# Two-layer streaming trunk: order of the second gate's products and stores, priority of the last block's evictions, place of the last transposes, start of the weight ring

## The chip, the cores and the metric

The kernel runs on one core of a Trainium2 chip as one program. The metric is the device time of one execution in microseconds (us), given as the median of several runs. Engines are named as in the profile: PE is the matrix engine, PEld its weight loads, DVE the vector engine, ACT the scalar engine, POOL the GpSimd engine, and SP the queue that issues most DMAs.

## The reference, cut to what matters

The trunk has two layers on 1024 positions of 1024 channels, in float32. Layer 0 mixes tokens with an S5 state-space mixer and a GLU, layer 1 with a short gated convolution. After each mixer come a SwiGLU feed-forward network with 2816 hidden units and a gated embedding:

```python
def swiglu_ffn(u, w_in, w_out):
    gate, up = jnp.split(u @ w_in, 2, axis=-1)
    return (jax.nn.silu(gate) * up) @ w_out

h = x
for i in range(DEPTH):
    hn = rmsnorm(h, norm_mix_g[i])
    mix = s5_mixer(hn, ...) if i % N_MIXERS == 0 else shortconv_mixer(hn, ...)
    h = h + mix
    h = h + swiglu_ffn(rmsnorm(h, norm_ffn_g[i]), ffn_w_in[i], ffn_w_out[i])
    gate = jax.nn.sigmoid(rmsnorm(h, norm_ple_g[i]) @ ple_w_gate[i])
    h = h + gate * (p[i] @ ple_w_up[i])
return rmsnorm(h, final_norm_g)
```

## The kernel before

**Products.** Every float32 operand is kept as two reduced-precision halves, high and low. `split` makes them: ACT casts the high half (L90), DVE subtracts it from the source (L91). One product of two operands is three matmuls (`mm3`, L124 to L126). On top of that the feed-forward input product works on 2x2 blocks with seven block products instead of eight (`block_product`). Product i of a block uses operand i of seven weight operands, and twelve matmuls. The seven results are added up in three PSUM tiles and in SBUF: L362 copies product 0 out on ACT, and DVE evicts products 1, 2, 4, 5 and 6 in L366, L370, L374, L376 and L378. Products 4, 5 and 6 start over in a PSUM tile that L366, L370 and L374 have emptied; they wait for those.

**Stages.** After the S5 mixer and the GLU (to about 400 us) comes the feed-forward input of layer 0, called f0: 22 blocks, in eleven pairs (one gate of a pair is `product(j)`, the other `product(j + NK)`). Then comes its output product `ffn_out`, then the gated embedding, the convolution, and the same feed-forward for layer 1, f1.

**A pair's hidden values.** Each pair yields seven operands for the output product. `store` splits one into a tile `hs` of a ring of four (tag by tag in turn) and sends it to DRAM (`hw`) with a DMA of POOL's queue (L473). Stores 0 and 1 belong to the first block of the pair. Stores 2, 6, 3, 4 and 5 belong to the second. Store 2 needs `u0`, which the seventh product completes (L378); store 6 needs `u1`, which the sixth completes (L376). With four tiles, store 5 takes the tile of the store that stands four places ahead of it in the text.

**The hand-over to the output product.** The last of the 22 blocks runs with `beside`: between its products, two generators (`make`) turn raw rows of the output weights into the operands of the first group of `ffn_out`, on ACT and DVE. Each makes four subtractions (L537, L541, L546, L549); the first generator does them on DVE, the second on POOL. The operands lie in `ulow` and `uhigh`, over the activations that the block has finished with. `ffn_out` takes its hidden values back from DRAM in chunks, four tiles `s8t` in turn, and the rows of `h` likewise; the list `queued` keeps these loads in one order on SP. The tiles of `s8t` and `h` lie where the ring of nine weight operands `ws` and the `hs`, `ev` and `kept` tiles lie, so a load waits until the last user of that place is done.

**`ffn_out`.** Six groups of hidden blocks are taken in turn, for four quarters of the positions each: `prod` multiplies, and `add` (L611, DVE) or `add_slow` (ACT copy, then POOL add at L620) adds the result to `h`. DVE adds run under `first()`, a scheduler priority.

**Transposes ahead of the blocks.** When `h` of the last tiles is normed, PE transposes it (L187) and DVE makes differences from it (`others`, L231 to L246) for the block operands. Ahead of f0 and ahead of the convolution the eight transposes of the last tile are kept in `held`, and `block_product` ties them behind a matmul of product 0 of the first block, so that they don't stand ahead of it on PE.

**What sets the order.** The order on each engine is found by a scheduler when the program is built. It takes the program text, its own estimates of durations and the priorities. So an edit in one place can move rows of another.

Of the kernel before, what the change touches and what calls it, by code (L numbers as in the profile page):

```python
# [14 lines left out]
ALU = mybir.AluOpType  # L15
# [9 lines left out]
def trunk(  # L25
# [317 lines left out]
    def block_product(ws, on_c11=None, beside=None):  # L343


        def prod(ps, i, start):
# [4 lines left out]
            if beside:  # L351
                beside(i)

        a = psum()
        prod(a, 0, True)
        product = next(i for i in reversed(tc.nc.cur_bb.bb.instructions) if i.engine == PE.engine)
        while held:
            tc.add_manual_dep(held.pop(), product.name,
                              mybir.DependencyInfo(mybir.DependencyClass.NoSync, mybir.DependencyReason.DATA),
                              reason="behind the first product")  # L360
        s1 = ev_tile("s1")
# [3 lines left out]
        u2 = ev_tile("u2")  # L365
        V.tensor_tensor(u2, b, s1, ALU.add)  # L366
        c = psum()
        prod(c, 2, True)
        s5 = ev_tile("s5")
        V.tensor_tensor(s5, c, s1, ALU.add)  # L370
        prod(a, 3, False)
        c11 = a if on_c11 is None else on_c11(a)
        prod(b, 4, False)
        V.tensor_tensor(s5, b, s5, ALU.add)  # L374
        prod(c, 5, False)
        V.tensor_tensor(u2, c, u2, ALU.add)  # L376
        prod(b, 6, False)
        V.tensor_tensor(s1, b, s1, ALU.add)  # L378
        return c11, u2, s1, s5
# [78 lines left out]
    def ffn_in(l):  # L458
# [16 lines left out]
        for j in range(NK):  # L475
# [8 lines left out]
            g0, g1, u0, u1 = product(j + NK)  # L484
            V.tensor_tensor(u0, u0, g0, ALU.mult)
            store(j, 2, u0)
            A.activation(g1, g1, AF.Silu)
            V.tensor_tensor(u1, u1, g1, ALU.mult)
            V.tensor_tensor(a21, a21, u1, ALU.add)
            store(j, 6, u1)  # L490
            store(j, 3, a21)
            V.tensor_tensor(a11, a21, a11, ALU.subtract)
# [27 lines left out]

    def make(l, j, got, eng=None):
        eng = eng or V
        wout = ffn_w_out[l].rearrange("(ht p) n -> ht p n", p=P)
# [12 lines left out]
        yield  # L536
        eng.tensor_tensor(b12, b12, b11, ALU.subtract)  # L537
        unit(5, b12)
        yield
        unit(3, b22)  # L540
        eng.tensor_tensor(b22, b22, b12, ALU.subtract)  # L541
        unit(6, b22)
        yield
        unit(2, b21)
        yield
        eng.tensor_tensor(b11, b22, b11, ALU.subtract)  # L546
        unit(7, b11)
        yield
        eng.tensor_tensor(b21, b21, b22, ALU.subtract)  # L549
        unit(4, b21)  # L550
# [3 lines left out]
    def begin(l):  # L554
        units.clear()
        units.update({j: {} for j in range(NK)})
        queued.clear()
        gens = [make(l, j, units[j], G if j else V) for j in groups[0]]
        for g in gens:
            next(g)  # L560
        steps = {0: (0, 1, 0, 1), 2: (0, 1, 0, 1), 3: (0,), 4: (1, 0, 1)}

        def beside(i):
            for g in steps.get(i, ()):
                next(gens[g], None)
        return beside

    def ffn_out(l, post, following):
# [4 lines left out]
        def fetch(gi, q, js=None):  # L573
            got = chunks_of.setdefault((gi, q), {})
            for j in js or groups[gi]:
                n = turns[0]
                turns[0] += 1
                ch = s8t[(n + 3) % 4].rearrange("p l n -> p (l n)").rearrange("p (c l j) -> p c l j", c=8, l=2)
                late = 6 + n // 4 % 2
# [95 lines left out]
    def ple(l, units, post, ahead):  # L675
        more, makers = ple_units(l, 1, [room_new(i) for i in range(4)])
        for nb in range(2):
# [670 lines left out]
    def ffn_ple(l, last, ahead):  # L1348
        units, makers = ple_units(l, 0, [room_high(3), room_high(4), room_high(5), room_new(3)])
        ffn_out(l, posted(norm_ple_g[l], False), makers)  # L1350
# [8 lines left out]
    release()  # L1359
    ffn_pools = (("ws", (1, 9, 5)), ("st", 3), ("kept", 1), ("hs", (1, 4, 3)), ("ev", 7))  # L1360
    inner("f0", lambda: ffn_in(0), ffn_pools)
# [41 lines left out]
```

## Time and profile before

| what | value |
|---|---|
| median of three runs | 2295.64 us |
| lowest and highest run | 2291.78 and 2298.13 us |
| the profiled execution's own time | 2295.53 us |
| its span, first to last instruction | 2293.3 us |
| granted PE clock, mean over the span | 0.98 of full speed |
| PE busy | 2169.0 us (95%) |
| DVE busy | 1632.9 us (71%) |
| ACT busy | 902.5 us (39%) |
| POOL busy | 368.7 us (16%) |

Rows of the timeline read: start in us, length in us, engine, source line, operation, tiles out<-in, and in brackets the idle time just before on that engine and what ended it. A row with xN stands for N instructions in a row. In a list of waits, a row gives the engine and line that waited, what it waited for, the sum of the waits in us, how many, and the longest. Starts count from the first instruction of the span. A tile is named without its buffer number, and `s` and `u` stand for the block results (s1, s5, u2).

### The profile page before, as it was taken

Reading aid. Unit: us, or ns where it says so; the run is one execution under the profiler, and the core shown is the slowest. Engines: PE = TensorE matmul, PEld = TensorE weight load, DVE = VectorE, ACT = ScalarE, POOL = GpSimd, SP = SyncE. Lnnn points to the kernel's source line nnn. Section 1 sums busy time; section 2 is a strip of 40 time slices with the busy share of each in tenths; the row PEclk is TensorE's granted clock in tenths of the full one; section 3 lists DMA queues with packets and bytes.
Section 4 is the critical chain, followed back from the end, with each engine's and each line's share of the span. In section 5 each row is a group of like instructions: output and inputs, shape, how many; then the busy total and the mean of one; then the engine's idle time right before and its main releaser. Section 6 shows DMA issues by size and latency. Waiting matters only on the chain.

```text
span 2293.3 us, 27860 instructions
## 1 busy us (share of the span) xinstructions
PE 2169.0 (95%) x9989; PEld 1785.8 (78%) x9989; DVE 1632.9 (71%) x2744; ACT 902.5 (39%) x1725; POOL 368.7 (16%) x442
## 2 busy tenths in 40 slices
PE   6988999899999989999979999979999999799998
PEld 5776888688888867878868888868888888677787
DVE  7885325877777777786587776487777777767764
ACT  6654223444433433334343332154444444323442
POOL 2110001011111122342010000011111112224310
PEclk9999999899999999999989999989999999999999
DMA  8555201354544477664232234533545454866723
GB/s 247 152 133 148 81 19 65 101 161 142 164 139 150 153 249 287 239 244 146 97 106 83 92 92 147 202 129 121 166 143 166 137 167 164 309 231 233 258 69 114
DMA packets 234010, 358.14 MB, mean 156 GB/s; under 512 B 23696, under 2 KB 166032, under 8 KB 233872
## 3 DMA queue, kind: packets, MB, share of 16 engines
q1 hardware_dynamic: 203040, 247.24, 33.3%
q0 software_dynamic: 30432, 109.08, 14.0%
q8 instruction: 79, 1.29, 0.2%
q14 instruction: 59, 0.48, 0.1%
q10 hardware_dynamic: 400, 0.04, 0.0%
HBM read 225.53 MB, written 114.29 MB: 148 GB/s over the span
## 4 chain that ended last, share of the span: by engine, by line
PE 63%; issue 14%; DVE 13%; DMA 6%; POOL 2%; ACT 1%; SPq 1%; DVEq 0%; POOLq 0%; ACTq 0%
PE psmm L124 20%; PE psmm L126 20%; PE psmm L125 20%; DVE h L611 2%; DMA raw<-in_ffn_w_out_dram 2%; DVE ulow L91 2%; POOL hw L473 2%; DVE uhigh L91 1%; DMA tw<-tmp 1%; DMA w<-hw 1%; DMA hw<-hs 1%; DVE W L844 1%; DVE gv L1194 1%; DVE tmp L844 1%; PE pstr L204 1%
## 5 line engine op out<-in xcount | busy, mean ns | idle before, releaser
L124 PE MATMUL psmm<-ulow,ws 128*128 128x512 f32 x896 | 353.4, 395 | 12.3 <-ACT ulow L90 9.8
L125 PE MATMUL psmm<-ulow,ws 128*128 128x512 f32 x896 | 353.3, 394 | 2.5 <-DVE ulow L91 2.5
L126 PE MATMUL psmm<-ulow,ws 128*128 128x512 f32 x896 | 352.7, 394 | 2.0 <-DVE ws L91 2.0
L124 PE MATMUL psmm<-uhigh,ws 128*128 128x512 f32 x672 | 262.1, 390 | 6.1 <-DVE s L374 4.5
L126 PE MATMUL psmm<-uhigh,ws 128*128 128x512 f32 x672 | 261.5, 389 | 0.0
L125 PE MATMUL psmm<-uhigh,ws 128*128 128x512 f32 x672 | 261.5, 389 | 0.0
L473 POOL DMA_DIRECT2D hw<-hs x154 | 116.1, 754 | 739.0 <-DVE hs L91 711.1
L611 DVE TENSOR_TENSOR h<-psmm,h 128x512 f32<-128x512 f32 x236 | 157.7, 684 | 76.6 <-PE psmm L126 42.0
L124 PEld LDWEIGHTS psmm<-ulow,ws 128*128 128x128 f32 x896 | 170.7, 191 | 48.9 <-ACT ulow L90 10.7
L90 ACT CAST ws<-raw 128x512 fp32r<-128x512 f32 x224 | 138.4, 621 | 174.8 <-PE psmm L126 166.8
L125 PEld LDWEIGHTS psmm<-ulow,ws 128*128 128x128 f32 x896 | 170.8, 191 | 39.3 <-DVE ulow L91 3.5
L126 PEld LDWEIGHTS psmm<-ulow,ws 128*128 128x128 f32 x896 | 170.8, 191 | 39.1 <-DVE ws L91 3.0
L620 POOL TENSOR_TENSOR h<-part,h 128x512 f32<-128x512 f32 x100 | 145.8, 1462 | 261.7 <-ACT part L619 220.2
L124 PE MATMUL psmm<-ulow,w 128*128 128x512 f32 x376 | 150.4, 400 | 25.5 <-DVE h L611 22.0
L91 DVE TENSOR_TENSOR ws<-raw,ws 128x512 fp32r<-128x512 f32 x224 | 153.5, 688 | 9.2 <-ACT ws L90 9.1
L124 PEld LDWEIGHTS psmm<-uhigh,ws 128*128 128x128 f32 x672 | 126.2, 188 | 34.8 <-DVE s L374 5.7
L90 ACT CAST ws<-st 128x512 fp32r<-128x512 f32 x168 | 103.8, 618 | 122.2 <-PE psmm L126 111.8
L125 PE MATMUL psmm<-ulow,w 128*128 128x512 f32 x376 | 148.1, 394 | 0.0
L126 PE MATMUL psmm<-ulow,w 128*128 128x512 f32 x376 | 147.9, 393 | 0.0
L126 PEld LDWEIGHTS psmm<-uhigh,ws 128*128 128x128 f32 x672 | 126.2, 188 | 26.3
L125 PEld LDWEIGHTS psmm<-uhigh,ws 128*128 128x128 f32 x672 | 126.2, 188 | 25.9
L91 DVE TENSOR_TENSOR ws<-st,ws 128x512 fp32r<-128x512 f32 x168 | 116.0, 691 | 16.0 <-ACT ws L90 15.8
(271 smaller groups left out, 4446.4 us busy)
## 6 DMA issues: line engine op xcount, KB each, us to landing
hw<-hs POOLq DMA_DIRECT2D x154, 512.0 KB, 4.2
w<-hw SPq DMA_DIRECT2D x88, 768.0 KB, 5.6
raw<-in_ffn_w_in_dram SPq DMA_DIRECT2D x88, 512.0 KB, 4.1
raw<-in_ffn_w_out_dram SPq DMA_DIRECT2D x44, 512.0 KB, 7.3
hd<-h POOLq DMA_DIRECT2D x24, 512.0 KB, 3.0
h<-hd SPq DMA_DIRECT2D x24, 512.0 KB, 7.1
raw<-in_conv_w_in_dram SPq DMA_DIRECT2D x24, 512.0 KB, 3.9
w<-hw SPq DMA_DIRECT2D x88, 128.0 KB, 5.5
```

Of the source, the lines that this page charges most:

```text
L90: A.copy(hi, src)
L91: V.tensor_tensor(lo, src, hi.bitcast(F32), ALU.subtract)
L124: PE.matmul(ps, ahi, bhi, start=start, stop=False, skip_group_check=more)
L125: PE.matmul(ps, ahi, blo, start=False, stop=False, skip_group_check=more)
L126: PE.matmul(ps, alo, bhi, start=False, stop=stop, skip_group_check=more)
L204: PE.transpose(pt[:, c * P:(c + 1) * P], xn[:, c * P:(c + 1) * P], ident)
L473: nc.gpsimd.dma_start(out=hidden[j][:, :, c].rearrange("q p l j -> p q l j"), in_=hs.bitcast(F32))
L611: done["sum"] = V.tensor_tensor(h[t][:, cs], ps, h[t][:, cs], ALU.add).ins
L620: G.tensor_tensor(h[t][:, cs], part, h[t][:, cs], ALU.add)
L844: V.tensor_tensor(o, a, b, op)
L1194: V.tensor_tensor_scan(gv[:, g, 1:P], dec, sv[:, g, 1:P], 0.0, ALU.mult, ALU.add)
```

## The change

Five things change.

1. In `block_product`, the five DVE evictions are put under `first()` when the block has `beside`, which is the last block of f0 and of f1.
2. The held transposes are tied behind the seventh-last PE instruction of product 0, that is behind the sixth of its twelve matmuls, rather than behind the last.
3. In the second half of a pair, the multiplication that completes `u1`, and store 6, stand ahead of the multiplication of `u0` and store 2. Stores now go round the ring of four as 0, 1, 6, 2, 3, 4, 5, so that store 5 gets the tile of store 6 instead of that of store 2.
4. `make` has no engine argument any more: all four subtractions of both generators run on DVE.
5. The ring of weight operands starts at tile 1 instead of 5, and the chunk tiles and one set of rooms of the embedding's weights (`room_new`) are renumbered to match. The last block's seven operands are then tiles 4, 5, 6, 7, 8, 0, 1.

```diff
+        soon = first if beside else ExitStack
         a = psum()
         prod(a, 0, True)
-        product = next(i for i in reversed(tc.nc.cur_bb.bb.instructions) if i.engine == PE.engine)
+        product = [i for i in tc.nc.cur_bb.bb.instructions[-60:] if i.engine == PE.engine][-7] if held else None
         while held:
             tc.add_manual_dep(held.pop(), product.name,
...
         u2 = ev_tile("u2")
-        V.tensor_tensor(u2, b, s1, ALU.add)
+        with soon():
+            V.tensor_tensor(u2, b, s1, ALU.add)
...
             g0, g1, u0, u1 = product(j + NK)
-            V.tensor_tensor(u0, u0, g0, ALU.mult)
-            store(j, 2, u0)
             A.activation(g1, g1, AF.Silu)
             V.tensor_tensor(u1, u1, g1, ALU.mult)
             V.tensor_tensor(a21, a21, u1, ALU.add)
             store(j, 6, u1)
+            V.tensor_tensor(u0, u0, g0, ALU.mult)
+            store(j, 2, u0)
             store(j, 3, a21)
...
-    def make(l, j, got, eng=None):
-        eng = eng or V
+    def make(l, j, got):
...
-        eng.tensor_tensor(b12, b12, b11, ALU.subtract)
+        V.tensor_tensor(b12, b12, b11, ALU.subtract)
...
-        gens = [make(l, j, units[j], G if j else V) for j in groups[0]]
+        gens = [make(l, j, units[j]) for j in groups[0]]
...
-                ch = s8t[(n + 3) % 4].rearrange("p l n -> p (l n)").rearrange("p (c l j) -> p c l j", c=8, l=2)
+                ch = s8t[(n + 1) % 4].rearrange("p l n -> p (l n)").rearrange("p (c l j) -> p c l j", c=8, l=2)
...
-    ffn_pools = (("ws", (1, 9, 5)), ("st", 3), ("kept", 1), ("hs", (1, 4, 3)), ("ev", 7))
+    ffn_pools = (("ws", (1, 9, 1)), ("st", 3), ("kept", 1), ("hs", (1, 4, 3)), ("ev", 7))
```

Lines of the changed kernel are numbered a little higher: L366, L370 and L374 become L368, L373 and L378; L541, L546 and L549 become L546, L551 and L554; L611 becomes L616.

First place: DVE in the last block of f0, from the eviction of product 1 to that of product 4. `ulow` and `uhigh` rows are low halves of `ffn_out` operands, `hs` rows those of stores 0 and 1, `raw` rows the subtractions of `make`. Before:

```order
L366 TENSOR_TENSOR u_6891<-psmm,s_6876 128x512
L91 TENSOR_TENSOR ulow<-raw,ulow 128x512 x2
L91 TENSOR_TENSOR hs<-kept,hs 128x4x128
L91 TENSOR_TENSOR hs<-s_6747,hs 128x4x128
L541 TENSOR_TENSOR raw<-raw 128x512
L91 TENSOR_TENSOR ulow<-raw,ulow 128x512 x2
L370 TENSOR_TENSOR s_6920<-psmm,s_6876 128x512
L546 TENSOR_TENSOR raw<-raw 128x512
L91 TENSOR_TENSOR ulow<-raw,ulow 128x512
L549 TENSOR_TENSOR raw<-raw 128x512
L91 TENSOR_TENSOR ulow<-raw,ulow 128x512 x2
L91 TENSOR_TENSOR uhigh<-raw,uhigh 128x512
L374 TENSOR_TENSOR s_6920<-psmm,s_6920 128x512
```

The same stretch of the changed kernel:

```order
L368 TENSOR_TENSOR u_6891<-psmm,s_6876 128x512
L91 TENSOR_TENSOR ulow<-raw,ulow 128x512 x2
L91 TENSOR_TENSOR hs<-kept,hs 128x4x128
L91 TENSOR_TENSOR hs<-s_6747,hs 128x4x128
L546 TENSOR_TENSOR raw<-raw 128x512 x2
L373 TENSOR_TENSOR s_6920<-psmm,s_6876 128x512
L91 TENSOR_TENSOR ulow<-raw,ulow 128x512 x2
L551 TENSOR_TENSOR raw<-raw 128x512 x2
L91 TENSOR_TENSOR ulow<-raw,ulow 128x512 x2
L554 TENSOR_TENSOR raw<-raw 128x512 x2
L91 TENSOR_TENSOR ulow<-raw,ulow 128x512
L378 TENSOR_TENSOR s_6920<-psmm,s_6920 128x512
```

The eviction of product 2 now has seven rows ahead of it from the eviction of product 1 on, that row included, where it had eight. The eviction of product 4 has seventeen, where it had fifteen, since three subtractions have come over from POOL and a `uhigh` row has gone behind it.

Second place: DVE at the end of the same block, the last stores and the first addition of `ffn_out`, with the semaphores that each row waits for (DMASW are those of POOL's stores). `hs_6995` is store 6 before, `hs_6988` store 2, `hs_6999`, `hs_7004` and `hs_7009` stores 3, 4 and 5. Before:

```order
L91 TENSOR_TENSOR hs_6995<-s5_6920,hs_6995 128x4x128 [waits DMASW1_49,Activation_49]
L492 TENSOR_TENSOR kept_6671<-kept_6672,kept_6671 128x512 [waits DVE_49]
L91 TENSOR_TENSOR hs_6999<-kept_6672,hs_6999 128x4x128 [waits DMASW2_49,Activation_49]
L91 TENSOR_TENSOR hs_6988<-s1_6876,hs_6988 128x4x128 [waits DMASW7_49,Activation_49]
L91 TENSOR_TENSOR hs_7004<-kept_6671,hs_7004 128x4x128 [waits DMASW3_49,Activation_49]
L494 TENSOR_TENSOR s1_6876<-s1_6876,kept_6671 128x512 [waits DVE_49]
L91 TENSOR_TENSOR hs_7009<-s1_6876,hs_7009 128x4x128 [waits DMASW6_49,Activation_49]
L611 TENSOR_TENSOR h_7034<-psmm_7056,h_7034 128x512 [waits DMAHW7_49,PE_49]
```

In the changed kernel store 6 is `hs_6990` and store 2 `hs_6995`:

```order
L91 TENSOR_TENSOR hs_6990<-s5_6920,hs_6990 128x4x128 [waits DMASW7_49,Activation_49]
L498 TENSOR_TENSOR kept_6671<-kept_6672,kept_6671 128x512 [waits DVE_49]
L91 TENSOR_TENSOR hs_6999<-kept_6672,hs_6999 128x4x128 [waits DMASW2_49,Activation_49]
L91 TENSOR_TENSOR hs_6995<-s1_6876,hs_6995 128x4x128 [waits DMASW1_49,Activation_49]
L91 TENSOR_TENSOR hs_7004<-kept_6671,hs_7004 128x4x128 [waits DMASW3_49,Activation_49]
L500 TENSOR_TENSOR s1_6876<-s1_6876,kept_6671 128x512 [waits DVE_49]
L91 TENSOR_TENSOR hs_7009<-s1_6876,hs_7009 128x4x128 [waits DMASW4_49,Activation_49]
L616 TENSOR_TENSOR h_7034<-psmm_7056,h_7034 128x512 [waits DMAHW7_49,PE_49]
```

The rows stand in the same sequence (6, 3, 2, 4, 5, then the addition). What has moved is the wait of store 5: from semaphore 6, which store 2's DMA raises, to semaphore 4, which store 6's DMA raises. On POOL the stores of both kernels go out as 6, 3, 2, 4, 5.

Third place: PE at the start of the convolution's first block (the same happens in f0). `pstr` rows are the held transposes, `psmm_9646` is product 0, `psmm_9661` product 1. Before, the last three matmuls of product 0, the transposes and the first of product 1:

```order
L124 MATMUL psmm_9646<-ulow_81,ws_9618 128x512
L125 MATMUL psmm_9646<-ulow_81,ws_9618 128x512
L126 MATMUL psmm_9646<-ulow_81,ws_9618 128x512
L187 MATMUL pstr_9559<-ident_72,xn_9522 128x128 x4
L187 MATMUL pstr_9564<-ident_72,xn_9522 128x128 x4
L124 MATMUL psmm_9661<-ulow_81,ws_9626 128x512
```

In the changed kernel:

```order
L187 MATMUL pstr_9559<-ident_72,xn_9522 128x128 x4
L187 MATMUL pstr_9564<-ident_72,xn_9522 128x128 x4
L124 MATMUL psmm_9646<-ulow_81,ws_9618 128x512
L125 MATMUL psmm_9646<-ulow_81,ws_9618 128x512
L126 MATMUL psmm_9646<-ulow_81,ws_9618 128x512
L124 MATMUL psmm_9646<-ulow_81,ws_9618 128x512
L125 MATMUL psmm_9646<-ulow_81,ws_9618 128x512
L126 MATMUL psmm_9646<-ulow_81,ws_9618 128x512
L124 MATMUL psmm_9661<-ulow_81,ws_9626 128x512
```

The transposes have moved six matmuls earlier. The subtractions behind them on DVE have not moved in f0 as far as the one (L236) on which product 1 hangs; in the convolution the first of them (L234) has gone ahead of two `ws` rows, and L236 stands where it stood.

More of the change, by code (lines that the diff above doesn't have):

```diff
@@ L359, in block_product @@
                               mybir.DependencyInfo(mybir.DependencyClass.NoSync, mybir.DependencyReason.DATA),
-                              reason="behind the first product")
+                              reason="inside the first product")
         s1 = ev_tile("s1")
@@ L369, in block_product @@
         s5 = ev_tile("s5")
-        V.tensor_tensor(s5, c, s1, ALU.add)
+        with soon():
+            V.tensor_tensor(s5, c, s1, ALU.add)
         prod(a, 3, False)
@@ L373, in block_product @@
         prod(b, 4, False)
-        V.tensor_tensor(s5, b, s5, ALU.add)
+        with soon():
+            V.tensor_tensor(s5, b, s5, ALU.add)
         prod(c, 5, False)
-        V.tensor_tensor(u2, c, u2, ALU.add)
+        with soon():
+            V.tensor_tensor(u2, c, u2, ALU.add)
         prod(b, 6, False)
-        V.tensor_tensor(s1, b, s1, ALU.add)
+        with soon():
+            V.tensor_tensor(s1, b, s1, ALU.add)
         return c11, u2, s1, s5
@@ L540, in make @@
         unit(3, b22)
-        eng.tensor_tensor(b22, b22, b12, ALU.subtract)
+        V.tensor_tensor(b22, b22, b12, ALU.subtract)
         unit(6, b22)
@@ L545, in make @@
         yield
-        eng.tensor_tensor(b11, b22, b11, ALU.subtract)
+        V.tensor_tensor(b11, b22, b11, ALU.subtract)
         unit(7, b11)
         yield
-        eng.tensor_tensor(b21, b21, b22, ALU.subtract)
+        V.tensor_tensor(b21, b21, b22, ALU.subtract)
         unit(4, b21)
@@ L675, in ple @@
     def ple(l, units, post, ahead):
-        more, makers = ple_units(l, 1, [room_new(i) for i in range(4)])
+        more, makers = ple_units(l, 1, [room_new(i) for i in (2, 3, 0, 1)])
         for nb in range(2):
@@ L1348, in ffn_ple @@
     def ffn_ple(l, last, ahead):
-        units, makers = ple_units(l, 0, [room_high(3), room_high(4), room_high(5), room_new(3)])
+        units, makers = ple_units(l, 0, [room_high(3), room_high(4), room_high(5), room_new(1)])
         ffn_out(l, posted(norm_ple_g[l], False), makers)
```

## Prediction

> **What bounds the kernel now.** I read the page first, then the list of PE's waits, then the timelines of the two hand-overs from the feed-forward input to its output product.
>
> ```profile
> PE 2169.0 (95%) x9989; PEld 1785.8 (78%) x9989; DVE 1632.9 (71%) x2744; ACT 902.5 (39%) x1725; POOL 368.7 (16%) x442
> PE psmm L124 <- DVE h L611: 28.1, 16, 8.9
> PE psmm L124 <- ACT ulow L90: 9.8, 3, 3.6
> PE psmm L124 <- DVE s L374: 4.5, 3, 1.9
> ```
>
> PE is busy for 95% and the change takes no matmul away. Only PE's idle time can shrink, and the change can reach the three waits shown. The additions of `ffn_out` (L611) are the largest, and two of their sixteen waits hold most of it. Here is PE at the hand-over in f0, then the same two waits in f1:
>
> ```profile
> 834.32 0.50 PE L124 MATMUL psmm<-uhigh,ws 128*128 128x512 f32 x1 [0.33 <-DVE s L370]
> 839.24 0.50 PE L124 MATMUL psmm<-uhigh,ws 128*128 128x512 f32 x1 [1.90 <-DVE s L374]
> 855.26 0.80 PE L124 MATMUL psmm<-ulow,w 128*128 128x512 f32 x1 [8.92 <-DVE h L611]
> 855.86 0.63 PE L125 MATMUL psmm<-ulow,w 128*128 128x512 f32 x1
> 859.27 0.40 PE L124 MATMUL psmm<-ulow,w 128*128 128x512 f32 x1
> ...
> 1955.15 0.50 PE L124 MATMUL psmm<-uhigh,ws 128*128 128x512 f32 x1 [1.90 <-DVE s L374]
> 1971.22 0.80 PE L124 MATMUL psmm<-ulow,w 128*128 128x512 f32 x1 [8.95 <-DVE h L611]
> ```
>
> Product 5 waits 0.33 us for the eviction of product 2, product 6 waits 1.90 us for that of product 4, and `ffn_out` stands 8.92 us (8.95 in f1) at its first addition. After that pause the matmuls come 0.43 us apart for a while (855.86 to 859.27, eight intervals); the twelve of product 5 took 3.02 us (834.32 to 837.34, where the 1.90 began), 0.25 each. Nine matmuls at 0.43 instead of 0.25 cost 1.6 us; that is the price of a restart at a low granted clock.
>
> **Why the addition is late.** DVE, POOL and ACT in the same stretch:
>
> ```profile
> 825.93 0.69 DVE L366 TENSOR_TENSOR u<-psmm,s 128x512 f32<-128x512 f32 x1 [0.42 <-PE psmm L126]
> 828.34 1.78 DVE L91 TENSOR_TENSOR hs<-s,hs 128x512 fp32r<-128x512 f32 x1
> 830.65 3.01 DVE L91 TENSOR_TENSOR ulow<-raw,ulow 128x512 fp32r<-128x512 f32 x2
> 834.18 1.39 DVE L546 TENSOR_TENSOR raw<-raw 128x512 f32<-128x512 f32 x1
> 838.50 0.68 DVE L374 TENSOR_TENSOR s<-psmm,s 128x512 f32<-128x512 f32 x1
> 843.51 0.69 DVE L485 TENSOR_TENSOR s<-s,sg 128x512 f32<-128x512 f32 x1
> 844.11 0.69 DVE L91 TENSOR_TENSOR hs<-s,hs 128x512 fp32r<-128x512 f32 x1
> 853.92 0.69 DVE L91 TENSOR_TENSOR hs<-s,hs 128x512 fp32r<-128x512 f32 x1 [6.11 <-ACT hs L90]
> 854.53 2.08 DVE L611 TENSOR_TENSOR h<-psmm,h 128x512 f32<-128x512 f32 x3
> 864.96 0.69 DVE L611 TENSOR_TENSOR h<-psmm,h 128x512 f32<-128x512 f32 x1 [0.67 <-PE psmm L126]
> ...
> 831.19 1.31 POOL L546 TENSOR_TENSOR raw<-raw 128x512 f32<-128x512 f32 x1
> 845.10 0.78 POOL L473 DMA_DIRECT2D hw<-hs  x1 [10.08 <-DVE hs L91]
> 846.31 2.27 POOL L473 DMA_DIRECT2D hw<-hs  x3 [0.43 <-DVE hs L91]
> ...
> 853.27 0.62 ACT L90 CAST hs<-s 128x512 fp32r<-128x512 f32 x1 [7.16 <-DMA hw<-hs]
> ```
>
> The addition at 854.53 stands on DVE behind the low half of store 5 (853.92), that behind its cast on ACT (853.27), and that waited 7.16 us for a store's DMA to free the tile. Which one, and how long it took, the chain of waits says; the next rows are the landing times of store 6 (issued 845.10, and 1961.03 in f1), of the second `h` load (issued 848.89, rows of position tile 5) and of the two raw loads behind it, and the stretch as a whole:
>
> ```profile
> 847.08 6.09 DMA hw<-hs
> ...
> DMA to landing us min/median/max: 3.7/3.7/3.7
> ...
> DMA to landing us min/median/max: 3.4/3.4/3.4
> ...
> DMA to landing us min/median/max: 8.4/8.4/8.4
> ...
> DMA to landing us min/median/max: 10.0/10.2/10.4
> ...
> 845.00:862.00 17.00, 8.08 (x27) 6.20 (x27) 6.78 (x11) 1.24 (x2) 4.32 (x6) 0.70 0.93 336
> ```
>
> It was store 2, issued 847.08, landed 853.17. Store 6 is issued 2.0 us earlier and landed at 848.8, after 3.7 us.
>
> **The evictions and the subtractions.** DVE starts a 0.69 us row 0.60 after the last (843.51, 844.11). From 825.93 to 838.50 it ran fifteen rows, 12.57 us; at 0.60 they would be 9.0. The 3.6 us more lie in three places where POOL works on the same raw tiles: 1.78 instead of 0.69, 3.01 for two instead of 1.29, 1.39 instead of 0.69, together 3.5. With POOL's subtractions gone that time goes, and three rows more stand ahead, one fewer elsewhere: the eviction of product 4 has seventeen rows ahead, so it starts at 825.93 + 17 x 0.60 = 836.1, 2.4 us earlier. The eviction of product 2 has seven rows, 830.1, well before its consumer. So the 0.33 and the 1.90 go, and product 6 starts at 836.1 + 0.74 (the distance 838.50 to 839.24) = 836.9 instead of 839.24, 2.4 us earlier. Products 5 and 6 then follow one another without a gap. The priority itself (the first edit) does little: the eviction of product 4 still has all this ahead.
>
> **The wait of store 5.** All that follows moves with it: store 6 is issued at 845.10 - 2.4 = 842.7 and lands 3.7 later, at 846.4. From the landing of the awaited store (847.08 + 6.09 = 853.17) to PE's restart (855.26) it took 2.09: cast, low half, addition. So PE restarts at 848.5 instead of 855.26, 6.8 us earlier. In f1, 1961.03 - 2.4 + 3.4 + 2.1 = 1964.1 instead of 1971.22, 7.1 earlier. Of the 8.9 us pause some 4.5 are left, and I leave the slow restart behind it where it is. The nearest row is another pause, of 3.34 us, which was followed 1.3 us later by matmuls 0.43 apart:
>
> ```profile
> 1537.28 0.96 PE L124 MATMUL psmm<-ulow,ws 128*128 128x512 f32 x3 [3.34 <-ACT ulow L90]
> 1538.56 0.63 PE L124 MATMUL psmm<-ulow,ws 128*128 128x512 f32 x1
> 1538.99 0.63 PE L125 MATMUL psmm<-ulow,ws 128*128 128x512 f32 x1
> ```
>
> "TensorE: Matmul & The Clock Gate" of the Trainium skill, section "HAM oscillation — how this bites in real kernels", puts the limit at idle gaps of about 3.4 us. By that rule a pause of 4.5 us is still punished, and one that came out 1.1 us shorter would not be, which would make the sum 3.2 us smaller; this row has the loss at 3.34 already, so by the row neither would escape.
>
> What becomes late next: the load of `h` for tile 5 now waits for store 2, third in POOL's queue, issued about 1.6 after store 6 (0.75 each) at 844.7, landing 6.1 later at 850.8. The load takes 8.4, so 859.2; its first addition, at 864.96 before, would be wanted at 864.96 - 6.8 = 858.2. That takes back 1.0 us in each layer. The raw loads behind it land some 10.2 after about 851.5, at 861.7; their first user on DVE has L616 rows behind it, but PE wants these 15 matmuls later, about 863, which is even. Bounds of this giveback: 0 if the load is as quick as 7.4, and 3 if the DMA queues, 93% busy here, put each transfer back by 2 us more. The load of `h` for the first tile now waits for product 4 (end 834.0) instead of product 0; it would be there before 842.4, also at 8.4 us, six us ahead of its use. The other loads of the ring's new start wait for a product earlier or none. I take 1.0 each: 5.8 net in f0 and 6.1 in f1, in all 11.9. Lower bound: 2.4 - 0.4 each if the pause stays, 4; upper bound 13.9, and 3.2 more without slow restarts.
>
> **Inside f0 and f1.** One pair shows the same wait of store 5 in the middle:
>
> ```profile
> 705.62 0.69 DVE L91 TENSOR_TENSOR hs<-s,hs 128x512 fp32r<-128x512 f32 x1 [4.27 <-ACT hs L90]
> 706.97 0.50 PE L124 MATMUL psmm<-uhigh,ws 128*128 128x512 f32 x1 [0.67 <-DVE s L374]
> ```
>
> PE lost 0.67 there. That goes. The other pairs hide it, and the new order costs them nothing: the two multiplications only change places.
>
> **Transposes.** Ahead of f0, DVE without a pause; ahead of the convolution, PE's wait and the two differences:
>
> ```profile
> 401.30:419.70 18.40, 9.06 (x29) 6.29 (x30) 18.39 (x36) 11.21 (x22) 1.34 (x3) 0.70 0.40 125
> 1194.52 1.22 PE L124 MATMUL psmm<-ulow,ws 128*128 128x512 f32 x2 [3.55 <-ACT ulow L90]
> 1192.34 0.68 DVE L234 TENSOR_TENSOR T<-b,psmm 128x512 f32<-128x512 f32 x1
> 1193.13 0.69 DVE L236 TENSOR_TENSOR T<-pstr,T 128x512 f32<-128x512 f32 x1
> ```
>
> Ahead of f0 DVE is busy for 18.39 of 18.40 us and L236 keeps its place, so PE waits as before, only with the transposes done sooner: 0. Ahead of the convolution L236 keeps its place too; only the 0.79 instead of 0.60 between the two rows goes, and a little slack: 0.4. If DVE had stood waiting for the transposes, the 3.55 us would shrink by up to the 2.6 us of six slow matmuls (0.43 each); L236 keeping its place in a busy queue says it does not.
>
> **Sum.** The profiled execution took 2295.53, the median of the runs is 2295.64, so the sum stands for both. 11.9 + 0.7 + 0.4 = 13.0, less 0.5 for a few additions of `ffn_out` that the scheduler moved behind another DVE row: 2295.5 - 12.5 = 2283.
>
> **Rivals.**
> *Given back.* Transfers set the restart: the stretch from 845 to 862 moves 336 GB/s at a DMA share of 0.93, and a shorter pause asks for the same bytes sooner. If later loads eat the 4.4 us of the pause and only the 2.4 of the evictions stays, 2 x 2.4 + 0.7 + 0.4 = 5.9: 2289.6, within 0.3%. Against it: the stores also start 2.4 earlier.
> *No slow restart.* If a pause of 4.5 us no longer lowers the clock, another 1.6 us in each layer goes: 2279.8. The row at 1537.28 speaks against it: 3.34 us of idle time were enough there. For it speaks only that the low clock did not set in at once in that place.
> *It does nothing.* The priority leaves the evictions where they stood and DVE, not POOL, was the limit: then 2294. The seventeen rows at 0.60 speak against it.
> *Slower.* More rows on DVE, in another order, reach the additions of `ffn_out`. In the changed order 28 DVE rows in all (19 in layer 0, 9 in layer 1) have slipped ahead of an addition that they stood behind. If PE awaited each, they would cost 28 x 0.60 = 16.8 us: 2295.5 - 12.5 + 16.8 = 2299.8. It decides from 12.5 / 0.60 = 21 rows on. Against it: PE waits for L611 sixteen times in all, of 236 additions, so one slip or two would count.
>
> **Chances.** Forecast 0.60, given back 0.20, no slow restart 0.10, nothing 0.05, slower 0.05. A measurement of this kernel tells 0.3%, 6.9 us, from no change, so faster means below 2288.7: the forecast, the third and a third of the second, 0.77. Slower over 0.3% needs more than the last rival's full price, 0.04. The range goes from 2277 (no slow restart, and no giveback) to 2291 (little more than the evictions).
>
> **What would show it.** Right: the gap at L374 gone in both layers, PE's pause at L611 about 4.5 us, the cast of store 5 released by a store issued 842 to 843, no wait in the pair at 705. Wrong: the pause unchanged, or a new wait of PE at the addition of tile 5 or for a raw load of over 2 us, or PE's waits in `ffn_out` grown by more than 5 us.

## The result, and the profile after

The changed kernel takes 2278.68 us (median of four runs, 2278.05 to 2283.35), the kernel before 2294.87 us beside it (four runs). The ratio is 0.9934, with a 95% interval from 0.9914 to 0.9953, so it is faster by 0.47% to 0.86%. The ratios in this document are formed from all runs, so they can differ a little from the quotient of two medians. A second measurement of the same kernel (below) gave 2281.66 us and 0.9945. The profiled execution of the changed kernel took 2283.35 us itself, the slowest of its four, with a span of 2281.6 us. Beside the profiled span of before, 2293.3, that is 11.7 us less.

The page of the changed kernel and its list of PE's waits (us in total, times, longest) answer to the first rows of the prediction:

```profile
PE 2168.4 (95%) x9989; PEld 1783.1 (78%) x9989; DVE 1636.9 (72%) x2752; ACT 908.7 (40%) x1725; POOL 357.5 (16%) x434
PE psmm L124 <- DVE h L616: 20.1, 20, 4.4
PE psmm L124 <- ACT ulow L90: 10.3, 3, 4.3
...
PE psmm L124 <- DVE s L378: 0.4, 2, 0.2
```

PE is as busy as before (2169.0), so nearly all of the 11.7 us came out of its idle time. The wait for the additions has fallen from 28.1 to 20.1 us, its longest from 8.9 to 4.4; the wait for the eviction of product 4 (L374 before, L378 now) from 4.5 to 0.4. The wait of the kind `ulow` has not shrunk (9.8, now 10.3).

PE at the two hand-overs of the changed kernel, f0 and then f1:

```profile
836.32 0.50 PE L124 MATMUL psmm<-uhigh,ws 128*128 128x512 f32 x1 [0.20 <-DVE s L378]
847.67 0.79 PE L124 MATMUL psmm<-ulow,w 128*128 128x512 f32 x1 [4.25 <-DVE h L616]
848.26 0.63 PE L125 MATMUL psmm<-ulow,w 128*128 128x512 f32 x1
...
850.39 0.53 PE L124 MATMUL psmm<-ulow,w 128*128 128x512 f32 x1
850.76 0.39 PE L125 MATMUL psmm<-ulow,w 128*128 128x512 f32 x1
...
1955.72 0.50 PE L124 MATMUL psmm<-ulow,w 128*128 128x512 f32 x1 [4.43 <-DVE h L616]
```

Product 5 no longer waits, product 6 waits 0.20 instead of 1.90, and the pauses are 4.25 and 4.43 instead of 8.92 and 8.95. The slow restart has stayed: the seven steps from 847.67 to 850.76 took 3.09 us, about 1.5 more than at the 0.23 or so that the matmuls take ahead of the pause.

DVE, POOL and ACT at the same hand-over:

```profile
825.34 0.69 DVE L368 TENSOR_TENSOR u<-psmm,s 128x512 f32<-128x512 f32 x1 [0.65 <-PE psmm L126]
827.75 0.69 DVE L91 TENSOR_TENSOR hs<-s,hs 128x512 fp32r<-128x512 f32 x1
829.56 0.68 DVE L373 TENSOR_TENSOR s<-psmm,s 128x512 f32<-128x512 f32 x1
835.58 0.68 DVE L378 TENSOR_TENSOR s<-psmm,s 128x512 f32<-128x512 f32 x1
844.20 0.69 DVE L500 TENSOR_TENSOR s<-s,kept 128x512 f32<-128x512 f32 x1
846.32 0.69 DVE L91 TENSOR_TENSOR hs<-s,hs 128x512 fp32r<-128x512 f32 x1 [1.43 <-ACT hs L90]
846.93 2.08 DVE L616 TENSOR_TENSOR h<-psmm,h 128x512 f32<-128x512 f32 x3
857.74 0.69 DVE L616 TENSOR_TENSOR h<-psmm,h 128x512 f32<-128x512 f32 x1 [1.51 <-DMA h<-hd]
859.67 0.69 DVE L542 TENSOR_TENSOR raw<-raw 128x512 f32<-128x512 f32 x1 [1.24 <-DMA raw<-in_ffn_w_out_dram]
...
842.17 0.75 POOL L479 DMA_DIRECT2D hw<-hs  x1 [12.55 <-DVE hs L91]
843.38 2.24 POOL L479 DMA_DIRECT2D hw<-hs  x3 [0.45 <-DVE hs L91]
...
845.67 0.62 ACT L90 CAST hs<-s 128x512 fp32r<-128x512 f32 x1 [2.49 <-DMA hw<-hs]
```

From the eviction of product 1 to that of product 4 DVE now takes 835.58 - 825.34 = 10.24 us, where it took 12.57, though two rows more stand there. The low half of store 1, 1.78 us before, takes 0.69. Store 6 goes out at 842.17, and the cast of store 5 waits for its DMA 2.49 us instead of 7.16. The low half of store 5 waits 1.43 instead of 6.11, and the first addition follows at 846.93. The two waits for loads (1.51, 1.24) are new.

The landing times of store 6, of the second `h` load (tile 5, issued 850.29) and of the two raw loads behind it, and the stretch as a whole (PE, PEld, DVE, ACT, POOL busy; granted clock, DMA share, GB/s), all of the changed kernel:

```profile
DMA to landing us min/median/max: 3.4/3.4/3.4
...
DMA to landing us min/median/max: 7.3/7.3/7.3
...
DMA to landing us min/median/max: 9.0/9.1/9.2
...
842.00:858.00 16.00, 11.76 (x46) 9.31 (x45) 7.81 (x13) 1.83 (x3) 5.41 (x7) 0.89 0.97 330
```

Store 6 is down at 845.6 (842.17 + 3.4), just ahead of the cast at 845.67. The DMA engines are busier than before (0.97 for 0.93) at about the same rate.

The lengths of the stages in the profiles, worked out from the starts of PE's rows, are as follows (us). "Blocks" is from the first matmul of the first block to the first of `ffn_out`, "hand-over" from there to the restart after the pause, "rest" from the restart to the convolution's first block (f0) or to the end of the span (f1).

| profile | start to first block | f0 blocks | hand-over | rest | convolution | f1 blocks | hand-over | rest |
|---|---|---|---|---|---|---|---|---|
| before | 406.4 | 435.7 | 13.2 | 326.4 | 348.6 | 427.8 | 13.2 | 322.1 |
| after | 408.4 | 430.8 | 8.5 | 327.7 | 346.3 | 425.3 | 8.7 | 325.9 |
| e1_stores | 406.1 | 433.5 | 8.8 | 329.1 | 347.8 | 427.2 | 8.5 | 322.2 |
| e2_dve | 404.6 | 431.6 | 13.0 | 327.4 | 347.6 | 425.1 | 13.3 | 324.7 |
| e3_prio | 407.2 | 433.3 | 13.3 | 327.3 | 348.1 | 427.2 | 13.2 | 321.3 |
| e4_held | 406.5 | 433.3 | 13.3 | 327.9 | 346.1 | 427.5 | 13.1 | 321.9 |
| e5_ring | 407.9 | 436.1 | 13.3 | 327.7 | 347.2 | 427.4 | 13.3 | 322.1 |
| e6_stores_dve | 406.4 | 431.4 | 8.5 | 328.6 | 346.9 | 425.1 | 8.8 | 323.7 |
| e9_after_again | 411.6 | 430.6 | 8.5 | 328.8 | 347.8 | 425.2 | 8.7 | 322.7 |

The hand-overs fall into two groups, 13 us and 8.5 us, and the blocks of f1 too, 427 and 425 us. The blocks of f0 have three, of which more below. The first column, which no edit touches before its end, ranges over 7 us by itself, and the last column over 4.6; these two make most of the difference from one profile of a kernel to another.

### The profile page after: what moved, and what is told of

Its sections match the earlier page's. It is cut to its first block, busy times and chain, and to the rows that moved or that the text cites. A ratio compares the mean times of both kernels' runs of the same rounds, so it can differ in the third digit from the quotient of the medians.

```text
span 2281.6 us, 27871 instructions
## 1 busy us (share of the span) xinstructions
PE 2168.4 (95%) x9989; PEld 1783.1 (78%) x9989; DVE 1636.9 (72%) x2752; ACT 908.7 (40%) x1725; POOL 357.5 (16%) x434
## 4 chain that ended last, share of the span: by engine, by line
PE 39%; issue 36%; DVE 11%; DMA 6%; POOL 5%; ACT 1%; SPq 1%; POOLq 0%; DVEq 0%; ACTq 0%
PE psmm L124 12%; PE psmm L126 12%; PE psmm L125 12%; POOL hw L479 5%; DVE h L616 2%; DMA raw<-in_ffn_w_out_dram 2%; DVE ulow L91 2%; DVE uhigh L91 1%; DMA tw<-tmp 1%; DMA w<-hw 1%; DVE gv L1199 1%; DVE W L849 1%; DVE raw L546 1%; DVE tmp L849 1%; PE pstr L204 1%
## 5 line engine op out<-in xcount | busy, mean ns | idle before, releaser
L124 PE MATMUL psmm<-ulow,ws 128*128 128x512 f32 x896 | 352.2, 394 | 12.9 <-ACT ulow L90 10.3
L616 DVE TENSOR_TENSOR h<-psmm,h 128x512 f32<-128x512 f32 x236 | 158.0, 684 | 76.4 <-POOL h L625 37.1
```

Of the source, the lines that this page charges most:

```text
L124: PE.matmul(ps, ahi, bhi, start=start, stop=False, skip_group_check=more)
L616: done["sum"] = V.tensor_tensor(h[t][:, cs], ps, h[t][:, cs], ALU.add).ins
```

## The experiments

Each experiment is timed against the kernel before on the same chip. The theory on test is the prediction's: two things carry the gain, the tile that store 5 waits for (edit 3) and POOL's subtractions that slow DVE ahead of the eviction of product 4 (edit 4). The rivals say that another of the five edits does it, or that transfers take it back.

**The order of products and stores alone** (edit 3 on the kernel before).

```diff
-            V.tensor_tensor(u0, u0, g0, ALU.mult)
-            store(j, 2, u0)
...
             store(j, 6, u1)
+            V.tensor_tensor(u0, u0, g0, ALU.mult)
+            store(j, 2, u0)
```

> Only the order of the second gate's products and stores is changed. Theory (two separate terms at each hand-over, POOL's subtractions and the tile of store 5): PE's waits for the eviction of product 4 stay at 1.9 us in each layer, its pause at the first addition of the output product falls from 8.9 to about 4.6 us, the wait of 0.67 us in the pair at 705 us goes; the load of h for tile 5 comes about 0.9 us too late in each layer. Sum -4.4 x 2 - 0.7 + 1.8 = -7.7 us, ratio about 0.9966. Rival (the transfers, not the tile, set the restart): the pause shrinks but later waits eat it, -2 us or less, ratio 0.999 or above.

Measured: 2285.2 us beside 2294.86, ratio 0.9953 (0.9938 to 0.9968). PE and DVE at its hand-over in f0:

```profile
836.76 0.50 PE L124 MATMUL psmm<-uhigh,ws 128*128 128x512 f32 x1 [1.90 <-DVE s L374]
848.37 0.50 PE L124 MATMUL psmm<-ulow,w 128*128 128x512 f32 x1 [4.51 <-DVE h L611]
...
823.47 0.69 DVE L366 TENSOR_TENSOR u<-psmm,s 128x512 f32<-128x512 f32 x1 [0.42 <-PE psmm L126]
825.88 1.78 DVE L91 TENSOR_TENSOR hs<-s,hs 128x512 fp32r<-128x512 f32 x1
836.03 0.68 DVE L374 TENSOR_TENSOR s<-psmm,s 128x512 f32<-128x512 f32 x1
```

The pause is halved, in f1 too (4.26), while the wait of 1.90 and DVE's 12.56 us (823.47 to 836.03) stay as they were. So half of the pause was the tile of store 5, and that half does not depend on the evictions.

**The subtractions alone** (edit 4 on the kernel before).

```diff
-        gens = [make(l, j, units[j], G if j else V) for j in groups[0]]
+        gens = [make(l, j, units[j]) for j in groups[0]]
```

> Only the four subtractions of the second generator go from POOL to DVE. Theory: the waits for the evictions of products 2 and 4 (0.33 and 1.90 us) go in both layers, the pause at the first addition stays at about 8.9 us since store 5 still waits for store 2, everything moves 2.4 us earlier; -4.8 us, ratio about 0.998. Rival (priority did it, the subtractions cost DVE what they save): the waits for product 4 stay at 1.9 us or grow, 0 us, ratio 1.000.

Measured: 2290.42 us beside 2294.86, ratio 0.9985 (0.9973 to 0.9996), which is 0.9 to 6.2 us. The same places of its trace:

```profile
833.28 0.50 PE L124 MATMUL psmm<-uhigh,ws 128*128 128x512 f32 x1 [0.21 <-DVE s L374]
849.09 0.80 PE L124 MATMUL psmm<-ulow,w 128*128 128x512 f32 x1 [8.71 <-DVE h L611]
...
822.30 0.69 DVE L366 TENSOR_TENSOR u<-psmm,s 128x512 f32<-128x512 f32 x1 [0.42 <-PE psmm L126]
824.72 0.69 DVE L91 TENSOR_TENSOR hs<-s,hs 128x512 fp32r<-128x512 f32 x1
832.54 0.69 DVE L374 TENSOR_TENSOR s<-psmm,s 128x512 f32<-128x512 f32 x1
```

This is the mirror image: the wait goes (1.90 to 0.21), the pause stays (8.71). DVE takes 10.24 us from 822.30 to 832.54, with no row longer than 0.69, though it does more work. Everything that follows comes earlier with the evictions, and the pause keeps its length because the stores that it awaits move along.

**The priority alone** (edit 1).

```diff
-        V.tensor_tensor(u2, b, s1, ALU.add)
+        with soon():
+            V.tensor_tensor(u2, b, s1, ALU.add)
```

(and so for the other four evictions)

> Only the evictions of the last block get the scheduler's priority. Theory: the eviction of product 2 goes two rows forward and that of product 4 keeps its fifteen rows and the blocking by POOL, so 0.33 us goes and 1.90 us stays in each layer: -0.7 us at most, ratio 1.000. Rival (the priority did it): both waits go, -4.5 us, ratio 0.998.

Measured: 2296.97 us, ratio 1.0003 (0.9994 to 1.0012). PE's waits there:

```profile
PE psmm L124 <- DVE s L378: 4.6, 2, 2.3
```

L378 is the eviction of product 4 in this kernel. The two waits for it have grown from 1.9 to 2.3 us each, while PE's wait of 0.33 for the eviction of product 2 is gone. So the priority brought the eviction of product 2 forward and PE stood at product 4 instead. By itself it gains nothing.

**The transposes alone** (edit 2).

```diff
-        product = next(i for i in reversed(tc.nc.cur_bb.bb.instructions) if i.engine == PE.engine)
+        product = [i for i in tc.nc.cur_bb.bb.instructions[-60:] if i.engine == PE.engine][-7] if held else None
```

> Only the place of the held transposes is changed. Theory: DVE is busy without a pause there and the subtraction on which product 1 hangs keeps its place, so PE's waits of 2.9 us ahead of f0 and 3.6 us ahead of the convolution stay within 0.5: 0 us, ratio 1.000. Rival (the transposes set these waits): each shrinks by up to 2.6 us, -5 us, ratio 0.998.

Measured: 2293.08 us beside 2295.94, ratio 0.9987 (0.9978 to 0.9996): about 3 us, hardly more than a measurement tells. PE's wait ahead of the convolution, in this kernel, in the one with the order of stores and the subtractions only (e6_stores_dve, below), and in the one with the ring only (e5_ring):

```profile
1193.43 1.00 PE L124 MATMUL psmm<-ulow,ws 128*128 128x512 f32 x2 [2.85 <-ACT ulow L90]
```

```profile
1187.18 0.97 PE L124 MATMUL psmm<-ulow,ws 128*128 128x512 f32 x2 [2.70 <-ACT ulow L90]
```

```profile
1197.86 1.22 PE L124 MATMUL psmm<-ulow,ws 128*128 128x512 f32 x2 [4.26 <-ACT ulow L90]
```

Neither of the last two has this edit. The wait is 2.70 in one and 4.26 in the other, and it was 3.55 in before, so it varies from kernel to kernel by more than the 0.4 us that the prediction gave the edit. Ahead of f0 the wait is 2.77 here and was 2.87 before, so the rival of this experiment, up to 2.6 us at each place, is not seen there. Where the 3 us of this run come from, its trace does not show; that stays open.

**The ring's start alone** (edit 5).

```diff
-    ffn_pools = (("ws", (1, 9, 5)), ("st", 3), ("kept", 1), ("hs", (1, 4, 3)), ("ev", 7))
+    ffn_pools = (("ws", (1, 9, 1)), ("st", 3), ("kept", 1), ("hs", (1, 4, 3)), ("ev", 7))
```

(with the renumbered chunks and rooms)

> Only the start of the weight ring and the numbering that goes with it are changed. Theory: 0 us within 2, the pause at the first addition stays at 8.9 us; the third chunk is loaded some microseconds sooner and nobody waits for it. Rival (the ring frees the loads sooner and the output product runs with fewer waits): PE's idle time between the hand-over and the end of the output product falls by 2 us or more in each layer, ratio 0.998.

Measured: 2296.1 us, ratio 0.9998 (0.9987 to 1.001). The pauses are 9.07 and 9.05. By itself it does nothing that can be told from 0.

**Both carriers together** (edits 3 and 4, the two diffs above on one kernel).

```diff
+            V.tensor_tensor(u0, u0, g0, ALU.mult)
+            store(j, 2, u0)
...
+        gens = [make(l, j, units[j]) for j in groups[0]]
```

> The order of products and stores and the subtractions on DVE together, without the priority, the transposes and the ring. Theory: these two carry the whole change: pause at the first addition about 4.3 us in both layers, no wait for evictions over 0.3 us; -15 us against the kernel before, the same as the whole change, ratio about 0.9935. Rival (priority or ring are needed for the two to act together): -11 us or less, ratio 0.995 or above.

Measured: 2281.13 us beside 2295.94, ratio 0.9933 (0.992 to 0.9947). That is the whole change's ratio, without its other three edits. Its pauses are 4.24 and 4.56 us, its waits for the eviction of product 4 are 0.20. The two alone multiply to 0.9953 x 0.9985 = 0.9938: within the intervals they add up, and neither takes from the other.

**The changed kernel once more**, with no edit, on the chip of the last one and of the next.

> The changed kernel once more, beside the others: 2279 us, ratio 0.9934 within 0.001.

Measured: 2281.66 us beside 2295.94, ratio 0.9945 (0.9932 to 0.9957). That is just outside the 0.001 that I had allowed, and shows how far two measurements of one kernel can differ.

**Store 3 ahead of store 2** (the changed kernel; what has become late is the `h` load for tile 5, which waits for store 2).

```diff
             store(j, 6, u1)
+            store(j, 3, a21)
             V.tensor_tensor(u0, u0, g0, ALU.mult)
             store(j, 2, u0)
-            store(j, 3, a21)
```

> The whole change, with store 3 ahead of store 2 in the text, so that the load of h for tile 5 waits for store 3 instead of store 2. Theory (what is late after the change is that load and the raw loads behind it on SP): it is issued about 2.5 us sooner, DVE's waits of 1.5 us for it and of 1.2 us for the raw tile go, PE's waits of 1.0 us (f0) and 2.2 us (f1) shortly after the hand-over shrink; -2 us against the whole change. Rival (the DMA engines are full, so loads land when they did): 0 us against the whole change.

Measured: 2278.37 us, ratio 0.9924 (0.9911 to 0.9937). The load is issued at 847.0 now, 0.9 us after the first addition (846.1); in the changed kernel it was 850.3, 3.4 us after it (846.9). Its landing time, DVE's wait for it, and the stretch as a whole:

```profile
DMA to landing us min/median/max: 10.1/10.1/10.1
...
857.17 0.69 DVE L617 TENSOR_TENSOR h<-psmm,h 128x512 f32<-128x512 f32 x1 [1.60 <-DMA h<-hd]
...
841.00:857.00 16.00, 11.75 (x45) 9.17 (x44) 7.66 (x13) 1.93 (x4) 5.06 (x7) 0.89 0.97 338
```

The load starts sooner and takes 10.1 us instead of 7.3, so it lands no sooner and DVE waits 1.60 instead of 1.51. The 7.3 is the shortest of what this load took in the profiles with the order of the change (7.3 in after, 7.7 in e9_after_again, 9.1 in e11_gblate below); 10.1 is beyond all three. In f0 the transfers set its arrival, not the moment of issue. In f1 the wait is not there, but it is not there in e11_gblate either, so that is not shown to be this edit's. The time cannot be told from that of the change, since the intervals overlap.

**Five tiles for the stores** (on the kernel before: store 5 then gets the tile of store 1; one eviction tile is given up for the room).

```diff
-    ffn_pools = (("ws", (1, 9, 5)), ("st", 3), ("kept", 1), ("hs", (1, 4, 3)), ("ev", 7))
+    ffn_pools = (("ws", (1, 9, 5)), ("st", 3), ("kept", 1), ("hs", (1, 5, 3)), ("ev", 6))
```

> The kernel before, with five hs tiles instead of four and six evictions' tiles instead of seven to pay for them, so that store 5 takes a tile whose DMA ended long ago. Theory (the pause is the wait of store 5 for its tile): the low half of store 5 follows at once on the subtraction ahead of it, the pause at the first addition falls from 8.9 to about 2.8 us, the waits of 1.9 us for the evictions stay; later loads take back 1 to 2 us in each layer, so -8 to -10 us, ratio 0.996. Rival (the first addition waits for something else, the loads of h or of the chunks): the pause stays above 6 us.

Measured: 2283.72 us beside 2295.79, ratio 0.9945 (0.993 to 0.9961). PE at the restart in f0, and ACT's wait for the last combination ahead of the cast of store 5:

```profile
848.74 0.50 PE L124 MATMUL psmm<-ulow,w 128*128 128x512 f32 x1 [3.54 <-DVE h L611]
849.08 0.39 PE L125 MATMUL psmm<-ulow,w 128*128 128x512 f32 x1
...
ACT hs L90 <- DVE s L494: 1.8, 1, 1.8
```

With no tile to wait for, the pause is 3.54 us (3.59 in f1), and the cast is released by DVE's own row, no longer by a DMA. I had expected 2.8 and left out that DVE stands still while ACT makes the cast, some 0.7 us. So of the pause of 8.9 us a good 5 were the tile, and 3.5 are DVE's rows and one cast. The change as made gets 4.7 of the 5.4. Not all of the shorter pause need be gain: in f0 DVE then waits 3.60 us for the load of `h` for tile 5.

**Five tiles on the changed kernel.**

```diff
-    ffn_pools = (("ws", (1, 9, 1)), ("st", 3), ("kept", 1), ("hs", (1, 4, 3)), ("ev", 7))
+    ffn_pools = (("ws", (1, 9, 1)), ("st", 3), ("kept", 1), ("hs", (1, 5, 3)), ("ev", 6))
```

> The changed kernel with five hs tiles and six evictions' tiles. Theory (after the change the pause is only partly the tile, 1.4 us on DVE; the rest is DVE's queue, and the loads behind are limited by the DMA engines): the pause falls from 4.3 to about 2.8 us, the addition of tile 5 and the raw tile come as late as before, so within 1.5 us of the changed kernel, 2279 us. Rival (each microsecond of pause is one of time): -3 us, 2276 us.

Measured: 2277.9 us beside 2295.79, ratio 0.9922 (0.9908 to 0.9935). The pauses are 3.60 and 3.58, another 0.7 to 0.9 shorter, and in f0 DVE waits for no load at the hand-over. Whether it beats the change is not settled: the intervals overlap.

**The gain's load later, by the text** (the load of the next norm's gain, L159, is issued right behind store 5 and shares the DMA engines with the `h` load).

```diff
-        gb = load_gain(gain)
+        gbs = [] if late else [load_gain(gain)]
...
+                if (gi, q) == (3, 0):
+                    post.load()
```

> The changed kernel, with the load of the next norm's gain (512 KB, on POOL's queue right behind store 5) moved from the hand-over to the fourth group of the output product. Theory (the loads behind the hand-over are limited by bytes: 97% busy, about 330 GB/s): 0.5 MB less is 1.6 us, DVE's waits of 1.5 us for the load of h and of 1.2 us for the raw tile shrink to under 0.5 us, about 1 us of PE's time in each layer: -2 us against the changed kernel. Rival (POOL's and SP's loads do not share a limit): those waits stay, 0 us.

Measured: 2282.39 us, ratio 0.9941 (0.9927 to 0.9955). The experiment failed in its aim: nothing holds the load back, so the scheduler put it behind store 5 as before. It is one more run of the change, and in f0 its waits for the two loads were 3.1 and 0.5, where the profile of after has 1.5 and 1.2.

**The gain's load tied** behind POOL's last addition of the third group.

```diff
+                if (gi, q) == (3, 0):
+                    behind = next(i for i in reversed(tc.nc.cur_bb.bb.instructions) if i.engine == G.engine)
+                    post.load()
+                    tc.add_manual_dep(next(i for i in reversed(tc.nc.cur_bb.bb.instructions) if i.engine == G.engine), behind.name,
...
```

> The changed kernel, with the load of the next norm's gain (512 KB) now tied behind POOL's last addition of the third group, so that it leaves the hand-over. Theory (the loads behind the hand-over are limited by bytes at 97% busy and about 330 GB/s): 0.5 MB less is 1.6 us; the load of h for tile 5 and the raw tile land about 1.5 us sooner after the restart, DVE's waits of 1.5 and 1.2 us for them shrink to under 0.5 us in both layers, about 1 us of PE's time each: 2278 us, ratio 0.9932. Rival (latency and order of the queues set these landings, not bytes): the waits stay over 1 us, as in the changed kernel, ratio 0.994.

Measured: 2279.41 us beside 2295.47, ratio 0.993 (0.9914 to 0.9946). The load now goes out at 964 us. The landing times of the `h` load for tile 5 and of the raw loads, and the first of DVE's waits behind the restart:

```profile
DMA to landing us min/median/max: 6.3/6.3/6.3
...
DMA to landing us min/median/max: 7.2/7.2/7.3
...
DVE h L623 <- PE psmm L126: 6.0, 4, 2.8
```

The `h` load takes 6.3 instead of 7.3, the raw loads 7.2 instead of 9.1, and DVE waits for neither in f0. Both are shorter than in each of the three profiles of the change (7.3 to 9.1 and 9.1 to 10.1). So the lateness behind the restart comes from the bytes in flight. The stage "rest" of f0 takes 327.1 us here, as long as with the long pause (327.3, below); so what these loads cost is 1 us or so in f0, too little to show in the time.

## Why the prediction was right, point by point

- **The evictions.** Seventeen rows at 0.60 were to take 10.2 us; they took 10.24. The wait of product 6 went from 1.90 to 0.20, where I had said none. From the eviction of product 1 to the restart it is 22.33 us (825.34 to 847.67) instead of 29.33, 7.0 less where I said 6.8 for both terms together. e2_dve shows that the subtractions shorten the way to the eviction of product 4, and e3_prio that the priority does not.
- **The tile of store 5.** Cause and size held: a pause of some 4.5 us was forecast, 4.25 and 4.43 came, and store 6 landed after 3.4 us (forecast 3.7). e1_stores and e8_hs5 show it, each by another way of freeing the tile.
- **The slow restart** stayed, as forecast, at about 1.5 us (forecast 1.6). The rival that took it away falls.
- **Given back.** The step held in its sum and not in its parts. I gave 1.0 to the load for tile 5 and called the raw loads even; DVE waited 1.51 and 1.24 in the profile of after, and 3.1 and 0.5 in e11_gblate, which has the same order. One number in that step is a slip: store 2 was to go out "about 1.6 after store 6", but the 844.7 that follows is 2.0 after it, and 2.0 came (842.17 to 844.1). What PE lost of it is seen in the stage "rest" of f0: its mean over the five profiles with the long pause (before, e2 to e5) is 327.3 us, over four with the short one (after, e1, e6, e9) 328.6. That is 1.2 us, close to the 1.0; in f1 the spread of single profiles hides it. The rival in which transfers eat the whole pause (2289.6) falls, but e7_order63 (in f0) and e12_gbtied show its mechanism at a small scale: the transfers in flight set when these loads arrive.
- **The transposes.** 0.4 was forecast. The wait ahead of the convolution was 4.26 with the change and 3.55 before, and it varies between 2.52 and 4.48 in kernels without the edit and between 2.85 and 4.26 in kernels with it; e4_held's 3 us have no row to stand on. Nothing is shown either way.
- **Slower by slipped rows.** PE now waits for additions 20 times instead of 16. The eighteen beside the two pauses make 20.1 - 4.25 - 4.43 = 11.4 us, where the fourteen beside the two of before made 28.1 - 8.92 - 8.95 = 10.2. That is about 1 us more, not 16.8, and even the 1 us is not shown to be the change's: e4_held, which moves only the transposes, waits 19 times, and the seventeen beside its two pauses make 12.4 us.
- **The sum.** Forecast 12.5 us less. The profiled execution has 12.2 less (2295.53 to 2283.35). The medians have 16.2 less and in the second measurement 14.3; the ratios, 0.9934 and 0.9945, come to 15.1 and 12.6. So it is not shown that the kernel gained more than was forecast. The stages that the two edits reach bear the forecast out. Beside the mean of e3_prio and e4_held, blocks and hand-over together are 7.4 us shorter in f0 (446.6 to 439.2) and 6.5 in f1 (440.5 to 434.0) in the two profiles of the changed kernel, where 6.8 and 7.1 were forecast. The three small terms of the sum (0.7 for the pair, 0.4 for the transposes, 0.5 for slipped rows) are shown by no run as costs or gains of the change. They come to only 0.6 of the 12.5, and that the 0.7 came out is luck (below).

**Inside f0** the step was half right. I took the 0.67 us in the pair at 706 for a cost of the old order that the new one takes away. The wait behind it is there: with the old order store 5 waits for its tile in all ten pairs. So ACT, in before, from 420 to 836 us (us in total, times, longest):

```profile
ACT hs L90 <- DMA hw<-hs: 41.1, 10, 6.8
```

The same window of e1_stores has no such row. But PE hides these waits nearly whole, and 0.67 is no fixed price. Of the five profiles with the old order and four tiles, before has two waits of PE in the pairs (0.67, and 1.00 at 678) and e5_ring has the same two (0.80 and 0.99); e2_dve, e3_prio and e4_held have none. In e3_prio and e4_held ACT waits for the stores too (35.2 and 29.3 us), and DVE's rows around that pair stand in the same order as in before. Accordingly the blocks of f0 take 435.7 and 436.1 us in before and e5_ring, and 433.3 in e3_prio and e4_held. So of the 4.9 us by which they are shorter in after than in before, some 2.4 are not shown to be the change's, and the forecast's 0.7 came out because the profile of before happened to have that wait. Taking the 41 us of waits from ACT gains nothing else that the profiles show.

## What to carry to other kernels

When a store waits for a tile of a ring, look up which earlier store holds that tile and how late it goes out: here it was enough to let an early store take the place of a late one, with no engine doing less. A light engine's help can cost more than it gives: POOL's three subtractions took 3.5 us from DVE, and DVE did them itself for 1.8. Apply each edit of a bundle by itself before building on it; of five here, two carried the gain, as far as these runs can tell, and of a wait that is hidden (41 us on ACT) next to nothing comes back.

## What the runs showed of the hardware

**The clock after a pause.** In before the granted clock was 1.00 in the twelve matmuls of product 5 (834.32 to 837.34) and 0.50 in the slow ones behind the pause (855.26 to 859.27). At the hand-overs, all 24 pauses of 4.24 us and more were followed by slow matmuls, but there is no sharp limit below. The changed kernel and e7_order63 both have a pause of 2.22 us in f1. In the changed kernel the matmuls went to steps of 0.43 us some 1.6 us later:

```profile
1985.93 0.50 PE L124 MATMUL psmm<-uhigh,w 128*128 128x512 f32 x1 [2.22 <-DVE h L616]
1986.26 0.40 PE L125 MATMUL psmm<-uhigh,w 128*128 128x512 f32 x1
...
1987.50 0.63 PE L124 MATMUL psmm<-ulow,w 128*128 128x512 f32 x1
1987.93 0.63 PE L125 MATMUL psmm<-ulow,w 128*128 128x512 f32 x1
```

In e7_order63 they did not:

```profile
1985.63 0.50 PE L124 MATMUL psmm<-uhigh,w 128*128 128x512 f32 x1 [2.22 <-DVE h L617]
1985.96 0.39 PE L125 MATMUL psmm<-uhigh,w 128*128 128x512 f32 x1
...
1987.35 0.39 PE L125 MATMUL psmm<-ulow,w 128*128 128x512 f32 x1
1987.58 0.40 PE L126 MATMUL psmm<-ulow,w 128*128 128x512 f32 x1
```

Three more profiles have a pause of 2.22 us at an addition: it was followed by slow matmuls in e1_stores and by none in e4_held and e11_gblate. The 3.54 us of e8_hs5 in f0 cost nothing either (0.34 and then 0.23 or 0.24 a step), its 3.59 in f1 did, and so did the 3.60 and 3.58 of e10_hs5_after. The Trainium skill, "TensorE: Matmul & The Clock Gate", section "HAM oscillation — how this bites in real kernels", warns of idle gaps of over about 3.4 us. The pauses of 4.25 us agree; those of 2.22 and that of 3.54 show that the length of the pause alone does not decide it.

**DVE beside POOL.** The low half of store 1 took 1.78 us in before and in e1_stores, and 0.69 in e2_dve; the row is the same, and POOL's subtraction of two tiles in SBUF beside it (827.97 to 829.57 in before) is gone. The Trainium skill, "SBUF — State Buffer", section "Who interferes with whom", has a DVE instruction with two SBUF inputs contend with a GpSimd instruction that reads SBUF; these rows agree.

**Full DMA engines.** At a share of 0.97 or so the `h` load for tile 5 took 10.1 us where it was issued earlier (e7_order63), and 7.3, 7.7 and 9.1 in the three profiles of the change. With one load of 512 KB less beside it (e12_gbtied) it took 6.3, and the raw loads 7.2 instead of 9.1 to 10.1.
